# A fused decoder block on one core: the down bias moved into each expert's matmuls, the overflow table moved ahead of the last down projection, and three engines tied to the issue order

## The chip, the core and the metric

The kernel runs on one core of one Trainium2 chip. TensorE multiplies, VectorE (DVE in the rows) and ScalarE (ACT) do elementwise work, GpSimd (POOL) here issues the transfers that add into the output, and SyncE (SP) issues the loads of the weights. The metric is the device time of one execution in microseconds (us); lower is better.

## The reference

One decoder block on 512 tokens of width 1024, in float32: a gated linear recurrence and a sliding-window attention in parallel, merged and projected, and then a mixture of experts. The change touches only the experts:

```python
logits = xf @ w_router + b_router                  # 32 experts
top_vals, top_idx = lax.top_k(logits, 4)
gates = softmax(top_vals)
# for each expert e and the tokens xb that chose it:
hu = xb @ w_up[e] + b_up[e]                        # 1024 -> 2048
x_glu = minimum(hu[:, ::2], 7.0)
x_lin = clip(hu[:, 1::2], -7.0, 7.0)
act = x_glu * sigmoid(1.702 * x_glu) * (x_lin + 1.0)
y = act @ w_down[e] + b_down[e]                    # 1024 -> 1024
out[token] += g2 * gate[token, e] * y
```

All 32 experts' weights are read once: 256 MB (MB of 1024 KB here) of `w_up` and 128 MB of `w_down`, in float32.

## The kernel before, in words

The first 445 us or so hold the recurrence, the attention, the projections and the router. The rest, the stage of the experts, is a Python loop that is unrolled: at step `e` it runs the up projection of expert `e` and then the down projection of expert `e-1`.

A **weight tile** is 128 x 2048 float32 (1 MB). An expert has 12: up tiles k = 0 to 7 and down tiles j = 0 to 3. SyncE loads each into one of 12 slots. All but down tile 3 are then split in two float16 halves in one of 6 further slots: ScalarE writes the high half (L341), VectorE the low half (L342), and TensorE needs both. The names in the rows are those of the slots (`slot`, `slotb`, `slotc`, with a number), the split's target on the left of the arrow and the loaded tile on the right. The 6 targets go round, so the split of a tile waits until TensorE has finished with the sixth split tile before it. `ahead(i)` (L1044) issues the splits up to six tiles ahead of the matmuls.

For one expert TensorE runs, in the program's order: for k = 0 to 7 the 48 matmuls of `up_k` (L1139) on four PSUM banks `pu0` to `pu3`, in groups f = 0 to 15, four to a bank; ahead of k = 4, 5, 6 and 7 one of the four **select groups** (`pick`, L1100 and L1105: 16 matmuls each, the last with 4 more), which gather the tokens of the next expert with the 0/1 matrix `sel` that VectorE makes (L1119); then the down projection of the expert before, three tiles in float16 (L1175) and one in float32 (L1167), into `pd0` and `pd1`.

Between the two stand: `swiglu`, which takes the four banks through VectorE (L1148, L1150, L1151, L1155) and ScalarE (L1149, L1154) in two halves; `up_bias` (L1132), four ScalarE copies that write the up bias of the next expert into `pu0` to `pu3`, where the matmuls then add; and `finish`, in which VectorE scales the down result into the tile `y` (L1209, two operations) and GpSimd adds the rows of `y` into the output by an indirect transfer (L1179). `y` has one buffer.

The down bias of the kernel before is a product of its own. At step 27 `gates_T` transposes the gates of all tokens, and at steps 28 to 31, behind k = 1, `bias_rows` multiplies the gates of 128 tokens with the 32 rows of `b_down` (L1198, L1199), scales into `y` (L1200) and adds into the output. `overflow_table` makes, behind the last step but one, a table for experts with more than 96 tokens; the loop that reads it runs no iteration in these runs (`y` of L1209 is written 64 times, twice for each of 32 experts).

The order of each engine's instructions is not that of the program text: a scheduler sets it when the kernel is built, and each engine then takes its instructions in that order.

Of the kernel before, what the change touches and what calls it, by code (L numbers as in the profile page):

```python
# [21 lines left out]
D = 1024  # L22
# [19 lines left out]
def block_body(tc, x, c, positions, w_ada, b_ada, norm1_gain, w_in, lower_bound_logits, hg_norm_gain,  # L42
# [19 lines left out]
    with top:  # L62
# [869 lines left out]
        ge = moe.tile([128, NT, 2, NE], F32, name="ge")  # L932
# [66 lines left out]
        def gates(t):  # L999

            V.tensor_sub(gt[:, t], tv[:, t, 0:4], tv[:, t, 0:1].to_broadcast([128, 4]))
            A.activation(gt[:, t], gt[:, t], AF.Exp, accum_out=gs[:, t, 0:1])
            V.reciprocal(gs[:, t, 1:2], gs[:, t, 0:1])
            V.tensor_scalar(gt[:, t], gt[:, t], gs[:, t, 1:2], GS, op0=OP.mult, op1=OP.mult)
            V.tensor_mul(oh[:, t], oh[:, t], gt[:, t, :, None].to_broadcast([128, 4, NE]))
            V.tensor_reduce(ge[:, t, 0], oh[:, t].rearrange("p k e -> p e k"), axis=AX.X, op=OP.add)
            V.tensor_copy(aux[:, t, :, 1], ge[:, t, 0])
            V.tensor_sub(aux[:, t, :, 2], ge[:, t, 0], aux[:, t, :, 1])
            V.tensor_copy(ge[:, t, 1], ge[:, t, 0])
# [4 lines left out]
        SU = SW * SH2  # L1014

# [10 lines left out]
        def bias_dn():  # L1026
            st = ready.pop(("bdn",))
            A.activation(bd, st[:64, :1024], AF.Copy)
            V.tensor_sub(bd[32:64], st[32:64, :1024], bd[32:64])
            free(st)  # L1030
# [111 lines left out]
        def swiglu(hf, act, act32):  # L1142
            n = 4 * C
            gl, li = pu[hf][:, :n], pu[2 + hf][:, :n]
            g = moe.tile([128, n], F32, name="sg_g", bufs=2)
            s = moe.tile([128, n], F32, name="sg_s", bufs=2)
            l = act32.rearrange("p k c -> p (k c)") if hf else moe.tile([128, n], F32, name="sg_l", bufs=2)
            V.tensor_scalar(g, gl, 1.0 / SU, 7.0, op0=OP.mult, op1=OP.min)  # L1148
            A.activation(s, g, AF.Silu, scale=1.702)  # L1149
            V.tensor_scalar(l, li, -7.0 * SU, 7.0 * SU, op0=OP.max, op1=OP.min)  # L1150
            V.scalar_tensor_tensor(l, l, SU, s, op0=OP.add, op1=OP.mult)  # L1151
            nb = 2 if hf else 4
            hi, lo = (act[:, q, 4 * hf:4 * hf + nb].rearrange("p k c -> p (k c)") for q in range(2))
            A.activation(hi, l[:, :nb * C], AF.Copy, scale=SACT / SU)  # L1154
            V.scalar_tensor_tensor(lo, l[:, :nb * C], SACT / SU, hi, op0=OP.mult, op1=OP.subtract)  # L1155

        def new_act():

            return (moe.tile([128, 2, 6, C], F16, name="act", bufs=2),
                    moe.tile([128, 4, C], F32, name="act32", bufs=2))  # L1160

        def down_j(w, j, act, act32):
# [7 lines left out]
            for k in (2 * j, 2 * j + 1):  # L1170
                o = 1024 * (k % 2)
                for n, (pa_, pw) in enumerate(PASSES):
                    for u in range(2):
                        c0 = 2048 * pw + o + 512 * u
                        T.matmul(pd[u][:C, :], lhsT=act[:, pa_, k, :], rhs=w[:, c0:c0 + 512],  # L1175
                                 start=(k == 0 and n == 0), stop=False)
# [5 lines left out]

        gT = moe.tile([64, 2, S], F16, name="gT")

        def gates_T():

            for t in range(NT):
                T.transpose(pd[1][:64, 128 * t:128 * t + 128], ge[:, t].rearrange("p u e -> p (u e)"), ident)
            A.activation(gT[:, 0], pd[1][:64, :], AF.Copy)
            V.tensor_sub(gT[:32, 1], pd[1][:32, :], gT[:32, 0])  # L1190

        def bias_rows(t):

            tok = slice(128 * t, 128 * t + 128)
            y = moe.tile([128, D], F32, name="y")
            for u in range(2):
                sl = slice(512 * u, 512 * u + 512)
                T.matmul(pd[u], lhsT=gT[:, 0, tok], rhs=bd[:, sl], start=True, stop=False)  # L1198
                T.matmul(pd[u], lhsT=gT[:32, 1, tok], rhs=bd[:32, sl], start=False, stop=True)  # L1199
                V.scalar_tensor_tensor(y[:, sl], pd[u], 1.0 / GS, g2row[:, sl], op0=OP.mult, op1=OP.mult)  # L1200
            idx = moe.tile([128, 1], I32, name="idx", bufs=4)
            G.iota(idx, pattern=[[0, 1]], base=128 * t, channel_multiplier=1)
            add_out(y, idx, 128)
# [63 lines left out]
        open_banks()  # L1267
        first = prepare(0)
# [7 lines left out]
        for e in range(NEX + 1):  # L1276
            if e < NEX:
                xg, gate, idx = state[e]
                prep = prepare(e + 1) if e + 1 < NEX else iter(())
                for k in range(8):  # L1280
# [6 lines left out]
                    if k == 1 and e == NEX - NT - 1:  # L1287
                        gates_T()
                    if k == 1 and e >= NEX - NT:
                        bias_rows(e - (NEX - NT))  # L1290
            if e < NEX:
# [3 lines left out]
                for hf_ in range(2):  # L1295
                    swiglu(hf_, *acts[e])
            if e == 0:
                for b in range(4):
                    up_bias(bu[:, 1], b)
            if e > 0:  # L1300
                _, gate, idx = state.pop(e - 1)
                for j in range(4):
# [13 lines left out]
            if e == NEX - 1:  # L1316
                tables = overflow_table()
# [4 lines left out]
        with tc.For_i(0, nreg, 1) as it:  # L1322
# [39 lines left out]
            for hf_ in range(2):  # L1362
                swiglu(hf_, act, act32)
# [50 lines left out]
```

## Time and profile before

| what | value |
|---|---|
| median of 3 runs | 1549.35 us (1546.44 to 1549.44) |
| the profiled execution's own time | 1549.81 us |
| its span, first to last instruction | 1548.0 us |
| mean granted TensorE clock | 0.974 of full |
| busy share of the span | TensorE 91%, VectorE 84%, ScalarE 67%, GpSimd 17% |
| bytes moved by transfers | 478.54 MB, mean 309 GB/s over the span |

The profiled execution took 0.46 us more than the median, and 1.81 us more than its own span. In a row of the timeline the columns are the start in us, the duration (of the whole group, from the first start to the last end, where the row stands for several instructions), engine, line, operation, output and inputs, and the count; square brackets give the idle time ahead of it and what ended that.

### The profile page before, as it was taken

The numbers are of one execution on the slowest core, as the hardware profiler recorded it, in microseconds if no ns is written. First come the engines' busy times: TensorE is split into PE (matmuls) and PEld (weight loads), VectorE is DVE, ScalarE is ACT, GpSimd is POOL, SyncE is SP. The second block draws the span as 40 slices with busy tenths as digits, with TensorE's granted clock in tenths as the row PEclk, the third lists the DMA queues.
The fourth block names the chain that finished last, engine by engine and source line by source line (L and its number), as shares of the span: only waits on it lengthen the run. The fifth ranks groups of instructions, "written<-read, shape, count | busy, mean of one in ns | idle before, by whom it ended". The sixth has DMA issues, their size and how long they took to land. (4 is left out here: it accounts for less than half of the span.)

```text
span 1548.0 us, 41016 instructions
## 1 busy us (share of the span) xinstructions
PE 1405.2 (91%) x18156; PEld 1038.0 (67%) x18156; DVE 1299.1 (84%) x1470; ACT 1039.7 (67%) x1023; POOL 266.2 (17%) x89
## 2 busy tenths in 40 slices
PE   3979999999979999999999999999999999877675
PEld 2536566445468888788878877777777777666562
DVE  6876676867889999999989898989999989786765
ACT  4555335433469988888788787887877787755551
POOL 1020000011110462000334311112211112111221
PEclk9989999999989999999999999999999999988888
DMA  9812321667569999999999999999999999988761
GB/s 316 281 59 82 110 55 55 187 252 276 206 255 378 396 411 405 408 408 403 407 400 401 389 385 388 396 392 393 387 384 401 394 400 389 378 303 309 277 233 15
DMA packets 114096, 478.54 MB, mean 309 GB/s; under 512 B 10781, under 2 KB 35450, under 8 KB 81114
## 3 DMA queue, kind: packets, MB, share of 16 engines
q1 hardware_dynamic: 106160, 458.78, 76.2%
q0 software_dynamic: 6016, 14.82, 4.6%
q8 instruction: 144, 2.36, 0.6%
q10 hardware_dynamic: 1738, 2.27, 0.4%
q14 instruction: 38, 0.31, 0.1%
HBM read 463.22 MB, written 16.79 MB: 310 GB/s over the span
## 5 line engine op out<-in xcount | busy, mean ns | idle before, releaser
L1179 POOL DMA_INDIRECT out_dram<-y,idx x36 | 230.5, 6402 | 823.8 <-DVE y L1209 780.3
L1139 PE MATMUL pu<-xg,slot 128*128 128x96 f16 x6192 | 292.1, 208 | 36.1 <-DVE slot L342 30.6
L1139 PEld LDWEIGHTS <-slot 128*128 128x128 f16 x6192 | 277.3, 99 | 50.5 <-DVE slot L342 34.3
L342 DVE SCALAR_TENSOR_TENSOR slot<-slot,slot 128x2048 f16<-128x2048 f32 (+1 forms) x111 | 250.5, 2265 | 31.0 <-ACT slot L341 29.0
L341 ACT ACTIVATE slot<-slot 128x2048 f16<-128x2048 f32 (+1 forms) x111 | 222.8, 2025 | 47.5 <-DVE slot L342 23.6
L1175 PEld LDWEIGHTS <-act 128*96 128x96 f16 x1152 | 138.8, 123 | 122.2 <-issue 25.0
L1139 PE MATMUL pu<-xg,slotc 128*128 128x96 f16 x4032 | 187.8, 206 | 3.6 <-DVE slotc L342 2.2
L1139 PEld LDWEIGHTS <-slotc 128*128 128x128 f16 x4032 | 177.1, 98 | 13.1 <-issue 5.7
L695 PE MATMUL mm<-hT,slot 128*128 128x512 f16 x672 | 152.5, 382 | 0.0
L342 DVE SCALAR_TENSOR_TENSOR slot<-slotb,slot 128x2048 f16<-128x2048 f32 x61 | 138.7, 2283 | 2.0 <-ACT slot L341 2.0
L1175 PE MATMUL pd<-slot,act 128*96 128x512 f16 x552 | 127.9, 379 | 10.0 <-DVE slot L342 9.6
L342 DVE SCALAR_TENSOR_TENSOR slotc<-slot,slotc 128x2048 f16<-128x2048 f32 x56 | 127.3, 2283 | 10.8 <-ACT slotc L341 9.2
L341 ACT ACTIVATE slot<-slotb 128x2048 f16<-128x2048 f32 x61 | 118.8, 1950 | 2.1 <-ACT xg L1107 1.4
L1100 PE MATMUL gb<-sel,h 128*128 128x96 f16 x2048 | 119.0, 207 | 0.7 <-ACT xg L1107 0.5
L695 PEld LDWEIGHTS <-slot 128*128 128x128 f16 x672 | 65.9, 99 | 78.4 <-issue 4.4
L341 ACT ACTIVATE slotc<-slot 128x2048 f16<-128x2048 f32 x56 | 115.0, 2074 | 1.2 <-PE pu L1139 1.1
L1139 PE MATMUL pu<-xg,slotb 128*128 128x96 f16 x2064 | 100.4, 208 | 11.3 <-DVE slotb L342 9.8
L1100 PEld LDWEIGHTS <-h 128*128 128x128 f16 x2048 | 100.9, 99 | 9.4 <-issue 2.2
L1107 ACT ACTIVATE xg<-gb 128x384 f16<-128x384 f32 x128 | 61.7, 483 | 64.1 <-PE gb L1105 33.6
L1139 PEld LDWEIGHTS <-slotb 128*128 128x128 f16 x2064 | 93.0, 99 | 16.0 <-DVE slotb L342 10.8
L1175 PE MATMUL pd<-slotc,act 128*96 128x512 f16 x408 | 95.2, 379 | 7.6 <-DVE slotc L342 5.4
L1149 ACT ACTIVATE sg_s<-sg_g 128x384 f32<-128x384 f32 x64 | 33.2, 519 | 101.6 <-DVE sg_g L1148 101.2
(334 smaller groups left out, 2137.0 us busy)
## 6 DMA issues: line engine op xcount, KB each, us to landing
slot<-in_w_up_dram SPq DMA_DIRECT2D x164, 1024.0 KB
slotb<-in_w_down_dram SPq DMA_DIRECT2D x98, 1024.0 KB
slotc<-in_w_up_dram SPq DMA_DIRECT2D x62, 1024.0 KB
slotb<-in_w_up_dram SPq DMA_DIRECT2D x30, 1024.0 KB
slot<-in_w_down_dram SPq DMA_DIRECT2D x30, 1024.0 KB
slot<-in_w_in_dram SPq DMA_DIRECT2D x16, 1024.0 KB
slot<-in_w_ada_dram SPq DMA_DIRECT2D x16, 1024.0 KB
slot<-in_w_ada_dram SPq DMA_DIRECT2D x16, 512.0 KB
```

What stands on the lines that cost most here:

```text
L341: A.activation(hi, src, AF.Copy, scale=SW)
L342: V.scalar_tensor_tensor(lo, src, SW, hi, op0=OP.mult, op1=OP.subtract)
L695: T.matmul(bk, lhsT=hl[:, o:o + 128], rhs=hT[:, ph, k, :], start=(k == 0 and n == 0), stop=(k == KT - 1 and n == 2))
L1100: T.matmul(bk[:, C * k:C * k + C], lhsT=h2[:, part, t, 128 * kk:128 * kk + 128], rhs=sel[:, t, :], start=(k == 0 and t == 0), stop=(t == N ...
L1107: A.activation(xg[:, part, 4 * u:4 * u + 4, :].rearrange("p k c -> p (k c)"), bk[:, :4 * C], AF.Copy)
L1139: T.matmul(o, lhsT=hl[:, 2048 * pw + 128 * f:2048 * pw + 128 * f + 128], rhs=xg[:, pa_, k, :], start=False, stop=(k == KT - 1 and n == 2), ...
L1149: A.activation(s, g, AF.Silu, scale=1.702)
L1175: T.matmul(pd[u][:C, :], lhsT=act[:, pa_, k, :], rhs=w[:, c0:c0 + 512], start=(k == 0 and n == 0), stop=False)
L1179: G.indirect_dma_start(out=out2, out_offset=bass.IndirectOffsetOnAxis(ap=idx[:n, :1], axis=0), in_=y[:n, :], in_offset=None, bounds_check= ...
```

## The change

Four things are changed in the text; the matrix sizes, the weight tiles, their loads and the slots stay.

1. The down bias. `gates_T` and `bias_rows` are gone. In their place `down_bias` starts each expert's down projection with two matmuls (one for `pd0`, one for `pd1`): the stationary operand is a column of a one-hot matrix `E64`, spread over the 96 tokens, the moving one the bias in float16 high and low parts. `E64` is made once.
2. `swiglu` is one function for both halves and issues its VectorE operations next to each other: both `g`, both `l`, both products, both low halves.
3. The overflow table stands ahead of the last down projection.
4. From `open_banks()` to the end of the experts, each instruction of VectorE, ScalarE and TensorE is tied to the one issued before it on its engine, so that the scheduler keeps the order of the program text on these three.

```diff
+        E64 = moe.tile([64, NE], F16, name="E64")
+        V.tensor_scalar(E64, iota_e[:64, :], pmod[:, 0:1], 32768.0, op0=OP.is_equal, op1=OP.mult)
...
-        def swiglu(hf, act, act32):
+        def swiglu(act, act32):
...
+            for hf in range(2):
+                g.append(moe.tile([128, n], F32, name="sg_g", bufs=2))
+                V.tensor_scalar(g[hf], pu[hf][:, :n], 1.702 / SU, 7.0 * 1.702, op0=OP.mult, op1=OP.min)
+                s.append(moe.tile([128, n], F32, name="sg_s", bufs=2))
+                A.activation(s[hf], g[hf], AF.Silu)
+            for hf in range(2):
+                l.append(act32.rearrange("p k c -> p (k c)") if hf else moe.tile([128, n], F32, name="sg_l"))
+                V.tensor_scalar(l[hf], pu[2 + hf][:, :n], -7.0 * SU, 7.0 * SU, op0=OP.max, op1=OP.min)
+            parts = []
+            for hf in range(2):
+                V.scalar_tensor_tensor(l[hf], l[hf], SU, s[hf], op0=OP.add, op1=OP.mult)
...
+                A.activation(hi, l[hf][:, :nb * C], AF.Copy, scale=SACT / SU)
+                parts.append((lo, l[hf][:, :nb * C], hi))
+            for lo, src, hi in parts:
+                V.scalar_tensor_tensor(lo, src, SACT / SU, hi, op0=OP.mult, op1=OP.subtract)
...
+        def down_bias(one):
+            for u in range(2):
+                T.matmul(pd[u][:C, :], lhsT=one.to_broadcast([64, C]), rhs=bd[:, 512 * u:512 * u + 512],
+                         start=True, stop=False)
...
-        def gates_T():
...
-        def bias_rows(t):
...
+        traced = nc.cur_bb.bb.instructions
+        marks = {}
+        mark = traced[-1]
...
-                    if k == 1 and e == NEX - NT - 1:
-                        gates_T()
-                    if k == 1 and e >= NEX - NT:
-                        bias_rows(e - (NEX - NT))
...
-                for hf_ in range(2):
-                    swiglu(hf_, *acts[e])
+                swiglu(*acts[e])
...
+            if e == NEX:
+                tables = overflow_table()
             if e > 0:
                 _, gate, idx = state.pop(e - 1)
+                down_bias(E64[:, e - 1:e])
...
-            if e == NEX - 1:
-                tables = overflow_table()
+        begin = next(n for n in reversed(range(len(traced))) if traced[n] is mark) + 1
+        for ins in traced[begin:]:
+            eng = ins.engine
+            if eng in (V.engine, A.engine, T.engine):
+                if eng in marks:
+                    tc.add_manual_dep(ins, marks[eng].name, mybir.DependencyInfo(
+                        mybir.DependencyClass.NoSync, mybir.DependencyReason.DATA), reason="order")
+                marks[eng] = ins
```

What the built programs hold, at three places. **First place**: ScalarE around `swiglu` of expert 18. `sg_s` is the sigmoid product, `act` the high half for the down projection, `pu` the bias copy, `xg` the copy of a select group, and L341 the high half of a weight tile. Before:

```order
L1149 ACTIVATE sg_s_14325<-sg_g_14324 128x384
L1132 ACTIVATE pu0_3492<-bu_2868 128x384
L341 ACTIVATE slot2_65<-slotb2_2808 128x2048
L1107 ACTIVATE xg_14610<-gb_14613 128x384
L1132 ACTIVATE pu2_3494<-bu_2868 128x384
L1149 ACTIVATE sg_s_14334<-sg_g_14333 128x384
L1132 ACTIVATE pu1_3493<-bu_2868 128x384
L341 ACTIVATE slot4_67<-slotb3_2809 128x2048
L1154 ACTIVATE act_14322<-sg_l_14326 128x384
L1132 ACTIVATE pu3_3495<-bu_2868 128x384
```

And in the change:

```order
L341 ACTIVATE slotc1_3486<-slot7_70 128x2048
L1113 ACTIVATE xg_14073<-gb_14283 128x384
L1155 ACTIVATE sg_s_14360<-sg_g_14358 128x384
L1155 ACTIVATE sg_s_14364<-sg_g_14362 128x384
L1164 ACTIVATE act_14356<-sg_l_14366 128x384
L1164 ACTIVATE act_14356<-act32_14357 128x192
L341 ACTIVATE slotc3_3488<-slot3_66 128x2048
L1138 ACTIVATE pu0_3494<-bu_2868 128x384
L341 ACTIVATE slotb1_2807<-slotb4_2810 128x2048
L1138 ACTIVATE pu1_3495<-bu_2868 128x384
L341 ACTIVATE slot2_65<-slot1_64 128x2048
L1138 ACTIVATE pu2_3496<-bu_2868 128x384
```

Two rows follow in the same pattern, a fourth tile and the copy into `pu3`. Before, the four bias copies stood among the steps of `swiglu`, with two tiles between the first and the last; now they stand behind it, each behind one more tile, and the tile ahead of `swiglu` is, counted in the order of use, up tile 1 of the next expert.

**Second place**: VectorE around `y` of expert 16 before and 17 in the change. `sel` is the 0/1 matrix of the select groups, L342 the low half of a weight tile. Before:

```order
L342 SCALAR_TENSOR_TENSOR slotc1_3484<-slot8_71,slotc1_3484 128x2048
L1209 SCALAR_TENSOR_TENSOR y_13827<-pd0_3496,gate_12327,g2row_2221 96x512
L1209 SCALAR_TENSOR_TENSOR y_13827<-pd1_3497,gate_12327,g2row_2221 96x512
L342 SCALAR_TENSOR_TENSOR slotc3_3486<-slot0_63,slotc3_3486 128x2048
L1119 TENSOR_TENSOR sel_15077<-iota_c_2845,pos_2851 128x384
L342 SCALAR_TENSOR_TENSOR slotb1_2807<-slot7_70,slotb1_2807 128x2048
```

And in the change:

```order
L342 SCALAR_TENSOR_TENSOR slot4_67<-slot5_68,slot4_67 128x2048
L1204 SCALAR_TENSOR_TENSOR y_14434<-pd0_3498,gate_12928,g2row_2221 96x512
L1204 SCALAR_TENSOR_TENSOR y_14434<-pd1_3499,gate_12928,g2row_2221 96x512
L342 SCALAR_TENSOR_TENSOR slot6_69<-slotc0_3485,slot6_69 128x2048
L342 SCALAR_TENSOR_TENSOR slotc1_3486<-slotc2_3487,slotc1_3486 128x2048
L1125 TENSOR_TENSOR sel_14542<-iota_c_2845,pos_2851 128x384
L342 SCALAR_TENSOR_TENSOR slotc3_3488<-slotb0_2806,slotc3_3488 128x2048
```

Between `y` and `sel` there is now a second tile, and the `sel` behind `y` of expert 17 is that of expert 20, whose first select group comes in the same step. Before, the `sel` behind `y` of expert 16 was that of expert 21: it stood two experts further ahead.

**Third place**: ScalarE where the experts begin, behind the router's last exponential (`gt`). Before:

```order
L1002 ACTIVATE gt_2857,gs_2858<-gt_2857 128x4
L341 ACTIVATE slotc1_3484<-slotb0_2806 128x2048
L1132 ACTIVATE pu0_3492<-bu_2868 128x384
L1132 ACTIVATE pu1_3493<-bu_2868 128x384
L1132 ACTIVATE pu2_3494<-bu_2868 128x384
L1132 ACTIVATE pu3_3495<-bu_2868 128x384
L1107 ACTIVATE xg_3516<-gb_3519 128x384
L341 ACTIVATE slotc3_3486<-slotb1_2807 128x2048
```

And in the change:

```order
L1002 ACTIVATE gt_2857,gs_2858<-gt_2857 128x4
L1113 ACTIVATE xg_3516<-gb_3519 128x384
L1113 ACTIVATE xg_3516<-gb_3537 128x384
L1113 ACTIVATE xg_3516<-gb_3555 128x384
L1113 ACTIVATE xg_3516<-gb_3573 128x384
L1138 ACTIVATE pu0_3494<-bu_2868 128x384
L1138 ACTIVATE pu1_3495<-bu_2868 128x384
L1138 ACTIVATE pu2_3496<-bu_2868 128x384
L1138 ACTIVATE pu3_3497<-bu_2868 128x384
L341 ACTIVATE slotc1_3486<-slotb0_2806 128x2048
```

The first tile of the stage (three were split earlier) stood ahead of these eight copies and now stands behind them; on VectorE five such tiles then stand ahead of `sel` of expert 1.

On TensorE the select groups of an expert, which before were cut in pieces and spread over the down projection and the first up tiles, now stand whole ahead of k = 4, 5, 6 and 7.

## Rows read from the trace of the kernel before

**Rows 1.** Windows: PE, PEld, DVE, ACT, POOL busy, clock, DMA share, GB/s.

```profile
541.00:571.00 30.00, 30.00 (x491) 24.50 (x489) 30.00 (x27) 26.38 (x24) 17.39 (x1) 1.00 1.02 408
...
980.00:1013.00 33.00, 31.68 (x503) 25.24 (x500) 30.22 (x26) 26.48 (x24) 5.88 (x1) 1.00 1.00 392
```

**Rows 2.** The timeline of GpSimd: the add into the output that ends an expert.

```profile
512.49 17.49 POOL L1179 DMA_INDIRECT out_dram<-y,idx  x1 [67.16 <-DVE y L1209]
...
980.85 5.88 POOL L1179 DMA_INDIRECT out_dram<-y,idx  x1 [27.05 <-DVE y L1209]
...
1310.47 5.41 POOL L1179 DMA_INDIRECT out_dram<-y,idx  x1 [27.04 <-DVE y L1209]
...
1522.87 5.50 POOL L1179 DMA_INDIRECT out_dram<-y,idx  x1 [28.40 <-DVE y L1209]
1534.04 1.42 POOL L1179 DMA_INDIRECT out_dram<-y,idx  x1 [5.67 <-DVEq L1322]
```

**Rows 3.** The waits from 1388 to 1432 us: sum, times, longest.

```profile
DVE y L1200 <- DMA out_dram<-y,idx: 7.9, 1, 7.9
```

**Rows 4.** The timeline of TensorE, with the products of the down bias.

```profile
1345.28 0.39 PE L1199 MATMUL pd<-bd,gT 32*128 32x512 f16 x1
1345.60 0.39 PE L1198 MATMUL pd<-bd,gT 64*128 64x512 f16 x1
...
1361.28 3.70 PE L1139 MATMUL pu<-xg,slot 128*128 128x96 f16 x44 [9.52 <-DVE slot L342]
```

**Rows 5.** The timeline of TensorE early in the stage.

```profile
544.22 0.84 PE L1100 MATMUL gb<-sel,h 128*128 128x96 f16 x16
544.90 2.20 PE L1139 MATMUL pu<-xg,slotc 128*128 128x96 f16 x48
546.94 0.84 PE L1100 MATMUL gb<-sel,h 128*128 128x96 f16 x16
...
552.38 0.85 PE L1100 MATMUL gb<-sel,h 128*128 128x96 f16 x16
...
566.48 2.20 PE L1139 MATMUL pu<-xg,slotb 128*128 128x96 f16 x48
```

**Rows 6.** The timeline of VectorE in a steady period.

```profile
1012.10 1.40 DVE L1209 SCALAR_TENSOR_TENSOR y<-pd,gate,g2row 96x512 f32<-96x512 f32 x2
1013.42 2.27 DVE L342 SCALAR_TENSOR_TENSOR slotc<-slot,slotc 128x2048 f16<-128x2048 f32 x1
1015.62 0.55 DVE L1119 TENSOR_TENSOR sel<-iota_c,pos 128x384 f16<-128x384 f32 x1
1016.09 2.28 DVE L342 SCALAR_TENSOR_TENSOR slotb<-slot,slotb 128x2048 f16<-128x2048 f32 x1
1018.29 0.15 DVE L1111 TENSOR_SCALAR idx<-gb 96x1 int32<-96x1 f32 x1
...
1018.62 2.29 DVE L342 SCALAR_TENSOR_TENSOR slot<-slot,slot 128x2048 f16<-128x2048 f32 x1
```

**Rows 7.** The timeline of TensorE behind VectorE's tile of 1016.09.

```profile
1018.42 2.04 PE L1139 MATMUL pu<-xg,slotb 128*128 128x96 f16 x44 [0.29 <-DVE slotb L342]
```

**Rows 8.** The timeline of ScalarE in the same period.

```profile
1021.67 4.12 ACT L341 ACTIVATE slotc<-slotc 128x2048 f16<-128x2048 f32 x2
...
1034.06 0.48 ACT L1132 ACTIVATE pu<-bu 128x384 f32<-128x384 f32 x1
1034.47 0.51 ACT L1149 ACTIVATE sg_s<-sg_g 128x384 f32<-128x384 f32 x1
...
1040.49 0.36 ACT L1154 ACTIVATE act<-act 128x192 f16<-128x192 f32 x1 [0.60 <-DVE act L1151]
1040.76 2.04 ACT L341 ACTIVATE slot<-slot 128x2048 f16<-128x2048 f32 x1
```

**Rows 9.** The timeline of ScalarE where the stage begins.

```profile
453.19 0.49 ACT L1107 ACTIVATE xg<-gb 128x384 f16<-128x384 f32 x1 [0.69 <-PE gb L1105]
```

**Rows 10.** The first line of the page.

```profile
span 1548.0 us, 41016 instructions
```

More of the change, by code (lines that the diff above doesn't have):

```diff
@@ L931, in block_body @@
         gs = moe.tile([128, NT, 2], F32, name="gs")
-        ge = moe.tile([128, NT, 2, NE], F32, name="ge")
+        ge = moe.tile([128, NT, NE], F32, name="ge")
         GS = 1024.0
@@ L1005, in gates @@
             V.tensor_mul(oh[:, t], oh[:, t], gt[:, t, :, None].to_broadcast([128, 4, NE]))
[L1006 to L1009, printed above, removed]
+            V.tensor_reduce(ge[:, t, :], oh[:, t].rearrange("p k e -> p e k"), axis=AX.X, op=OP.add)
+            V.tensor_copy(aux[:, t, :, 1], ge[:, t, :])
+            V.tensor_sub(aux[:, t, :, 2], ge[:, t, :], aux[:, t, :, 1])
         bu = moe.tile([128, NE, 16], F32, name="bu")
@@ L1014, in block_body @@
         SU = SW * SH2
+        pmod = moe.tile([64, 1], F32, name="pmod")
+        G.iota(pmod[0:32], pattern=[[0, 1]], base=0, channel_multiplier=1, allow_small_or_imprecise_dtypes=True)
+        G.iota(pmod[32:64], pattern=[[0, 1]], base=0, channel_multiplier=1, allow_small_or_imprecise_dtypes=True)
+        E64 = moe.tile([64, NE], F16, name="E64")
+        V.tensor_scalar(E64, iota_e[:64, :], pmod[:, 0:1], 32768.0, op0=OP.is_equal, op1=OP.mult)
+        SBD = 1.702 * SW * SACT / 32768.0
         def bias_up():
@@ L1027, in bias_dn @@
             st = ready.pop(("bdn",))
-            A.activation(bd, st[:64, :1024], AF.Copy)
-            V.tensor_sub(bd[32:64], st[32:64, :1024], bd[32:64])
+            A.activation(bd, st[:64, :1024], AF.Copy, scale=SBD)
+            V.scalar_tensor_tensor(bd[32:64], st[32:64, :1024], SBD, bd[32:64], op0=OP.mult, op1=OP.subtract)
             free(st)
@@ L1140, in up_k @@
                              start=False, stop=(k == KT - 1 and n == 2), skip_group_check=True)
-        def swiglu(hf, act, act32):
+        def swiglu(act, act32):
             n = 4 * C
[L1144 to L1155, printed above, removed]
+            g, l, s = [], [], []
+            for hf in range(2):
[9 more added lines that the diff above has]
+                V.scalar_tensor_tensor(l[hf], l[hf], SU, s[hf], op0=OP.add, op1=OP.mult)
+                nb = 2 if hf else 4
+                hi, lo = (act[:, q, 4 * hf:4 * hf + nb].rearrange("p k c -> p (k c)") for q in range(2))
+                A.activation(hi, l[hf][:, :nb * C], AF.Copy, scale=SACT / SU)
+                parts.append((lo, l[hf][:, :nb * C], hi))
+            for lo, src, hi in parts:
+                V.scalar_tensor_tensor(lo, src, SACT / SU, hi, op0=OP.mult, op1=OP.subtract)
         def new_act():
@@ L1175, in down_j @@
                         T.matmul(pd[u][:C, :], lhsT=act[:, pa_, k, :], rhs=w[:, c0:c0 + 512],
-                                 start=(k == 0 and n == 0), stop=False)
+                                 start=False, stop=False)
         def add_out(y, idx, n):
@@ L1181, in add_out @@
                                  compute_op=OP.add)
-        gT = moe.tile([64, 2, S], F16, name="gT")
-        def gates_T():
[L1187 to L1190, printed above, removed]
-        def bias_rows(t):
[L1194 to L1203, printed above, removed]
         def finish(gate, idx):
@@ L1361, in block_body @@
                 hl_give(slot)
-            for hf_ in range(2):
-                swiglu(hf_, act, act32)
+            swiglu(act, act32)
+            e1h = moe.tile([64, 1], F16, name="ovh")
+            V.tensor_scalar(e1h, pmod, col[:64, 0:1], 32768.0, op0=OP.is_equal, op1=OP.mult)
+            down_bias(e1h)
             for j in range(4):
```

## The prediction

> **What bounds the kernel now.** I read first the timeline of GpSimd, because the add into the output marks the end of each expert [rows 2]: 512.49 us for expert 0, 980.85 for expert 15, 1310.47 for expert 25, 1522.87 for expert 30 and 1534.04 for expert 31. So the stage has three parts. The first 15 periods take 31.22 us each (468.36 / 15). The next ten take 32.96 (329.62 / 10). The five after those take 42.48 (212.40 / 5).
>
> The windows say what is full [rows 1]. In 33 us of a steady period TensorE is busy for 31.68, VectorE for 30.22, ScalarE for 26.48, and the transfers are at 392 GB/s of the 408 that they reach early in the stage. So four resources lie close together, and what an order of the work does to their waits can decide.
>
> TensorE's own period follows from two kinds of spacing [rows 5]. A select group with its up tile takes 2.72 (544.22 to 546.94), an up tile 2.04 (544.90 to 546.94). From the fourth select group to the next expert's first up tile it is 14.10 (552.38 to 566.48): 0.68 select, 2.04 tile, 11.38 down projection. One expert without any wait is then 14.10 + 4 x 2.04 + 3 x 2.72 = 30.42.
>
> The last five periods are long for another reason. The waits show VectorE's `y` of the down bias (L1200) held for 7.9 us by the transfer that empties the one buffer of `y` [rows 3]. The low halves of the tiles stand behind it, so TensorE then waits 9.52 us for one, and its next 44 matmuls take 3.70 us [rows 4], against 2.04 for 44 in a steady period [rows 7].
>
> **The change, part by part.**
>
> *The down bias.* What goes is the excess of five periods: 212.40 - 5 x 32.96 = 47.6 us. What comes is two matmuls of 512 columns for each expert. The nearest row is the old product's spacing, 0.32 us (1345.28 to 1345.60) [rows 4], so 0.64 for two, and TensorE's own period becomes 31.06. The bounds are nothing (hidden in a wait) and twice 0.39, the row's duration. In the order below the price falls into a wait, so it hardly moves the sum. [...] The other part, making `E64` and scaling the bias, is a handful of operations ahead of the stage, less than what `gates_T` drops.
>
> *The tie to the text's order with the new `swiglu`.* This moves most. I follow one period, with 0 at the start of an expert's fourth select group. A hand-over between engines costs 0.05 (VectorE's tile ends at 1016.09 + 2.28 = 1018.37 [rows 6], TensorE starts at 1018.42 [rows 7]). The spacings are: VectorE's tile 2.20, `y` 1.32, an operation of 128 x 384 0.47, the three small ones behind the selects 0.33 [rows 6]; ScalarE's tile 2.0 (two in 4.12, ends overlapping by 0.08), bias copy 0.41, the last, half-sized `act` 0.27 [rows 8].
>
> 1. ScalarE's tile ahead of `swiglu` is up tile 1 of the next expert. By the rotation of six targets it waits for TensorE's up tile 6, which ends at 0.16, so it runs from 0.20 to 2.30. VectorE's low half runs from 2.34 and frees VectorE at 4.54. The three small operations take it to 4.87.
> 2. Two `g`, two `l` and two products follow, 0.47 apart. The last product starts at 7.22 and ends at 7.77. ScalarE's last `act` starts at 7.81, and ScalarE is free at 8.08.
> 3. Now four tiles, each followed by one bias copy: 4 x 2.41 = 9.64. The fourth tile runs from 15.31 to about 17.40, its copy into `pu3` ends at 17.78. TensorE has begun the next expert's up tile 0 at 14.10 + 0.64 = 14.74 and needs `pu3` three quarters through it, at 14.74 + 1.53 = 16.27. It waits until 17.83: **1.56 us**. Before, these copies stood among the steps of `swiglu`, with two tiles between the first and the last: 1034.06 and 1034.47 show one of them directly ahead of the sigmoid [rows 8], so no such wait stood there.
> 4. VectorE's low half of that fourth tile runs from 17.45 to 19.65, `y` to 20.97, two tiles to 25.37, `sel` ends at 25.92. TensorE, free of `pu3` at 17.83, does the last quarter of up tile 0 (0.51) and tiles 1 to 3 (6.12), stands at the first select group at 24.46 and waits until 25.97: **1.51 us**. Before, `sel` came one tile behind `y` [rows 6] and two experts further ahead.
> 5. Three select groups with tiles, 8.16, bring it to the next fourth select group: a period of **34.13 us** = 31.06 + 1.56 + 1.51.
>
> In this chain VectorE and ScalarE aren't full: each waits for the other or for TensorE once a round, and the ring closes through the six targets. It is a fixed order, so the period holds from the first expert to the last with select groups.
>
> *The start.* ScalarE's last copy for expert 0's tokens ends at 453.68 [rows 9]. In the changed order four bias copies stand ahead of the stage's first tile (four starts, 1.6, to 455.3), that tile ends at 457.3, five low halves on VectorE (11.1 with the hand-over) reach 468.4, `sel` 468.9. Only then can the first select group of expert 1 run. Three more with their tiles, 8.16, set the first zero of the count above at 477.1. In this one round the four bias copies stand together behind `act` (8.08 + 4 x 0.41 = 9.72), the next tile's high half is done at 11.8, and three low halves and `sel` on VectorE end at 19.0; three selects more, and the next zero is 27.2 later, 504.3. From there the count holds, and `y` of expert 0 ends 21.0 behind that, at 525.3; its add starts at about 525.6, 13 us later than now [rows 2].
>
> *The table and the end.* Expert 30 has no selects ahead of it: from 17.83, one quarter tile 0.51, seven tiles 14.28, bias 0.64, down 11.38 and `y` 1.37 bring it to 46.0, which is 25.0 behind the `y` before. Expert 31's bias waits for the first half of that `y`, then 0.64 + 11.38 + `y` make it 12.8 later, where now it is 11.17 [rows 2]. The table's VectorE work lies beside that down projection, which is longer than it; if it stood in the way instead, some 5 us would come on top. From the last add to the end of the span, 13.96 (1548.0 [rows 10] less 1534.04 [rows 2]), stays.
>
> *The sum.* 525.6 + 29 x 34.13 (989.8) + 25.0 + 12.8 + 13.96 = 1567.2 of span. The profiled execution took 1.81 more than its span and 0.46 more than the median, so this is 1568.5 on the median's scale; I say **1568**. In other words: 25 periods lose about 2.2 each (55), the last five give back 50, the start loses 13, the end about 1. Break-even would be a period of 33.5.
>
> **The rivals.**
>
> *One of the two waits doesn't come* (the other side). The second, for `sel`, is a race of 1.5 us between eight VectorE operations and four tiles on TensorE. For it: a single tile done earlier by VectorE removes it. Against: every spacing in it is a row of a steady period. The period is then 32.62, the time 1568 - 29 x 1.51 = 1524. It decides from 0.64 us less a period on.
>
> *TensorE's own work sets the period*, 31.06, with both waits hidden by the reserve of six split tiles: 1568 - 29 x 3.07 = 1479. For it: TensorE is the busiest of the four [rows 1]. Against: in the new order no reserve is left, since the tile in step 1 waits for TensorE itself. [...]
>
> *The granted clock falls behind the new waits.* After 9.52 us of waiting 44 matmuls took 3.70 instead of 2.04 [rows 4, 7]. If each expert paid that once, it would be 1.66 x 29 = 48 on top, 1616. Against: after a wait of 0.29 the 44 ran at full speed [rows 7], and the clock is 1.00 in both windows [rows 1].
>
> **How the numbers follow.** A measurement of this kernel can tell about 0.2%, 3.1 us, from no change. The forecast has 0.70, its own range being 1556 to 1582 (0.4 us on a period). One wait fewer: 0.12. TensorE's own period: 0.07. The clock: 0.06. The last 0.05 is a shortening that happens to meet the break-even. Slower is then 0.76 (forecast and clock), faster 0.19, same 0.05. The range that keeps 8 in 10 leaves out the clock, TensorE's period and the far half of the first rival: 1538 to 1584.
>
> **What would show it.** In the changed profile the adds should be 34.1 apart from the first expert on, expert 0's at about 525. In each expert TensorE should show a wait of about 1.6 for a bias copy on ScalarE and one of about 1.5 for `sel`. The waits of 8 to 10 us in the last four experts should be gone, with the clock at 1.00 there, and the transfers should run below 392 GB/s. I am wrong if VectorE gets to `sel` earlier than 1.4 us behind TensorE, or if the bias copies come while up tile 0 is still in its third quarter.

## The result, and the profile after

The changed kernel takes 1568.97 us (median of 4 runs, 1568.66 to 1572.76) against 1547.89 of the kernel before: a ratio of 1.0142, 95% interval 1.0121 to 1.0163. The forecast was 1568, with 0.76 for slower. The profiled execution has a span of 1567.3 us; the sum of the prediction was 1567.2.

The timeline of GpSimd, as in [rows 2], for experts 0, 1, 14, 15, 25, 29, 30 and 31:

```profile
529.40 3.41 POOL L1196 DMA_INDIRECT out_dram<-y,idx  x1 [83.56 <-DVE y L1204]
563.47 10.31 POOL L1196 DMA_INDIRECT out_dram<-y,idx  x1 [30.65 <-DVE y L1204]
...
1005.81 10.30 POOL L1196 DMA_INDIRECT out_dram<-y,idx  x1 [23.70 <-DVE y L1204]
1039.78 10.29 POOL L1196 DMA_INDIRECT out_dram<-y,idx  x1 [23.67 <-DVE y L1204]
...
1380.28 10.29 POOL L1196 DMA_INDIRECT out_dram<-y,idx  x1 [23.71 <-DVE y L1204]
...
1516.85 1.42 POOL L1196 DMA_INDIRECT out_dram<-y,idx  x1 [23.72 <-DVE y L1204]
1541.84 1.42 POOL L1196 DMA_INDIRECT out_dram<-y,idx  x1 [23.57 <-DVE cnt L1215]
1554.38 1.42 POOL L1196 DMA_INDIRECT out_dram<-y,idx  x1 [11.12 <-DVEq L1326]
```

There are no stages left: the first period is 34.07 us, a later one 33.97, and 29 periods take 987.45, or 34.05 each (predicted 34.13). TensorE's waits over those 29 periods (529 to 1517 us; sum, times, longest) name two causes and hardly anything else:

```profile
PE gb L1106 <- DVE sel L1125: 39.1, 29, 1.4
PE pu L1145 <- ACT pu L1138: 35.0, 29, 1.3
PE gb L1106 <- issue: 0.4, 1, 0.4
PE pu L1145 <- issue: 0.4, 1, 0.4
```

The waits for a late low half that the last experts had before, of which [rows 4] shows one of 9.52, are gone, and the windows of the last experts show the clock at 1.00 with transfers at 370 to 388 GB/s (columns as in [rows 1]):

```profile
1380.00:1414.00 34.00, 31.45 (x504) 25.23 (x501) 30.57 (x27) 26.97 (x24) 10.29 (x1) 1.00 0.99 388
1414.00:1448.00 34.00, 31.01 (x489) 24.64 (x486) 29.94 (x25) 26.33 (x23) 10.30 (x1) 1.00 0.96 370
```

So the end gave back what was forecast and every period lost what was forecast. One period of TensorE, VectorE and ScalarE (their timelines; the fourth select group starts at 984.63, which is the zero of the prediction's count):

```profile
984.63 0.84 PE L1106 MATMUL gb<-sel,h 128*128 128x96 f16 x16
...
987.61 0.63 PE L1176 MATMUL pd<-bd,E 64*96 64x512 f16 x2
988.17 2.79 PE L1192 MATMUL pd<-slot,act 128*96 128x512 f16 x12
...
999.41 1.69 PE L1145 MATMUL pu<-xg,slotb 128*128 128x96 f16 x36
1002.32 0.67 PE L1145 MATMUL pu<-xg,slotb 128*128 128x96 f16 x12 [1.22 <-ACT pu L1138]
1002.83 6.30 PE L1145 MATMUL pu<-xg,slot 128*128 128x96 f16 x144
1010.46 0.85 PE L1106 MATMUL gb<-sel,h 128*128 128x96 f16 x16 [1.33 <-DVE sel L1125]
```

```profile
989.52 1.01 DVE L1153 TENSOR_SCALAR sg_g<-pu 128x384 f32<-128x384 f32 x2
...
994.77 4.67 DVE L342 SCALAR_TENSOR_TENSOR slot<-slot,slot 128x2048 f16<-128x2048 f32 x2 [1.43 <-ACT slot L341]
...
1004.13 1.40 DVE L1204 SCALAR_TENSOR_TENSOR y<-pd,gate,g2row 96x512 f32<-96x512 f32 x2
...
1009.85 0.55 DVE L1125 TENSOR_TENSOR sel<-iota_c,pos 128x384 f16<-128x384 f32 x1
```

```profile
992.69 2.05 ACT L341 ACTIVATE slot<-slot 128x2048 f16<-128x2048 f32 x1
...
1001.78 0.49 ACT L1138 ACTIVATE pu<-bu 128x384 f32<-128x384 f32 x1
```

From the zero, `g` starts at 4.89 (predicted 4.87), the first of the four tiles at 8.06 (8.08), the copy into `pu3` ends at 17.64 (17.78), TensorE goes on at 17.69 (17.83), `y` starts at 19.50 (19.65), `sel` ends at 25.77 (25.92), and the first select group starts at 25.83 (25.97). The waits in brackets are shorter than the predicted 1.56 and 1.51 because the page counts idle time from the end that it gives for the matmul before, which lies 0.16 behind the next start where nothing waits (544.90 + 2.20 against 546.94 in [rows 5]). From start to start they are 1.38 (1002.32 less 999.41 + 1.53) and 1.51 (1010.46 less 1002.83 + 6.12); the first is 0.18 shorter than predicted.

### The profile page after: what moved, and what is told of

It is laid out like the page before. It is cut to its first block, busy times and chain, and to the rows that moved or that the text cites. A ratio compares the mean times of both kernels' runs of the same rounds, so it can differ in the third digit from the quotient of the medians.

```text
span 1567.3 us, 41129 instructions
## 1 busy us (share of the span) xinstructions
PE 1406.7 (90%) x18200; PEld 1036.1 (66%) x18200; DVE 1310.0 (84%) x1458; ACT 1052.6 (67%) x1022; POOL 331.5 (21%) x83
## 5 line engine op out<-in xcount | busy, mean ns | idle before, releaser
L1196 POOL DMA_INDIRECT out_dram<-y,idx x32 | 296.0, 9249 | 814.0 <-DVE y L1204 779.3
L1145 PE MATMUL pu<-xg,slot 128*128 128x96 f16 x6192 | 283.2, 207 | 25.5 <-ACT pu L1138 25.1
L342 DVE SCALAR_TENSOR_TENSOR slot<-slot,slot 128x2048 f16<-128x2048 f32 (+1 forms) x111 | 252.0, 2272 | 55.3 <-ACT slot L341 51.4
L1145 PEld LDWEIGHTS <-slot 128*128 128x128 f16 x6192 | 272.0, 98 | 36.4 <-issue 33.8
L341 ACT ACTIVATE slot<-slot 128x2048 f16<-128x2048 f32 (+1 forms) x111 | 224.3, 2022 | 51.8 <-DVE slot L342 22.9
L1106 PE MATMUL gb<-sel,h 128*128 128x96 f16 x2048 | 109.2, 207 | 49.3 <-DVE sel L1125 48.8
L342 DVE SCALAR_TENSOR_TENSOR slotc<-slot,slotc 128x2048 f16<-128x2048 f32 x56 | 128.3, 2292 | 27.0 <-ACT slotc L341 24.5
L342 DVE SCALAR_TENSOR_TENSOR slot<-slotb,slot 128x2048 f16<-128x2048 f32 x61 | 138.6, 2286 | 13.2 <-ACT slot L341 12.0
L341 ACT ACTIVATE slot<-slotb 128x2048 f16<-128x2048 f32 x61 | 118.9, 1953 | 26.8 <-PE pu L1145 23.8
L1106 PEld LDWEIGHTS <-h 128*128 128x128 f16 x2048 | 94.4, 98 | 54.5 <-DVE sel L1125 53.3
L1192 PE MATMUL pd<-slot,act 128*96 128x512 f16 x552 | 123.9, 380 | 0.0
L341 ACT ACTIVATE slotc<-slot 128x2048 f16<-128x2048 f32 x56 | 116.2, 2075 | 8.5 <-PE pu L1145 8.5
L695 PEld LDWEIGHTS <-slot 128*128 128x128 f16 x672 | 65.7, 98 | 77.7 <-issue 3.1
L342 DVE SCALAR_TENSOR_TENSOR slotc<-slotb,slotc 128x2048 f16<-128x2048 f32 x42 | 95.5, 2286 | 12.7 <-ACT slotc L341 12.3
L1145 PE MATMUL pu<-xg,slotb 128*128 128x96 f16 x2064 | 95.7, 206 | 6.2 <-ACT pu L1138 6.1
L1184 PE MATMUL pd<-slot,act 128*96 128x512 f32 x216 | 97.1, 592 | 0.0
L341 ACT ACTIVATE slotc<-slotb 128x2048 f16<-128x2048 f32 x42 | 81.8, 1953 | 17.4 <-PE pu L1145 16.1
```

Of the source, the lines that this page charges most:

```text
L341: A.activation(hi, src, AF.Copy, scale=SW)
L342: V.scalar_tensor_tensor(lo, src, SW, hi, op0=OP.mult, op1=OP.subtract)
L695: T.matmul(bk, lhsT=hl[:, o:o + 128], rhs=hT[:, ph, k, :], start=(k == 0 and n == 0), stop=(k == KT - 1 and n == 2))
L1106: T.matmul(bk[:, C * k:C * k + C], lhsT=h2[:, part, t, 128 * kk:128 * kk + 128], rhs=sel[:, t, :], start=(k == 0 and t == 0), stop=(t == N ...
L1145: T.matmul(o, lhsT=hl[:, 2048 * pw + 128 * f:2048 * pw + 128 * f + 128], rhs=xg[:, pa_, k, :], start=False, stop=(k == KT - 1 and n == 2), ...
L1184: T.matmul(pd[u][:C, :], lhsT=act32[:, k - 4, :], rhs=w[:, o:o + 512], start=False, stop=(k == KT - 1))
```

## The experiments

The theory is the prediction's: VectorE and ScalarE in the fixed order form a ring with TensorE, that is a chain of waits that comes back to its start in each period, and TensorE waits twice in it. The rivals are that TensorE's own work, with the two new matmuls, or the transfers set the 34.0, and that each wait stands for itself. Each group of kernels was timed beside the kernel before on the same chip.

**`sel` first.**

```diff
-PICK_AT = (2, 4, 5, 6, 7)
+PICK_AT = (0, 4, 5, 6, 7)
```

> Changed kernel with one number altered: `sel` of the next expert is issued ahead of up tile 0 instead of up tile 2, so that on VectorE it stands directly behind `y`. Theory (one ring of VectorE and ScalarE in a fixed order, TensorE waiting twice in it, 1.2 us for a bias copy and 1.3 us for `sel`): `sel` ends at 21.5 of the period, ahead of the 24.5 at which TensorE asks for it, the second wait goes and the first stays; the period falls from 34.0 to 32.5 and the time from 1569 to about 1525. Rival (the two added matmuls or TensorE's own work set the period): no change, 1569. Rival (the ring is set elsewhere, the wait only moves): 1560 to 1569.

Measured: 1525.0 us, ratio 0.9867 (0.9843 to 0.9892). TensorE's waits over 29 periods (521 to 1472 us) now name `sel` no more, and the other wait stays:

```profile
PE pu L1145 <- ACT pu L1138: 26.7, 28, 1.3
PE pu L1145 <- issue: 7.6, 18, 0.9
```

The time falls by 44 us when one instruction of 0.55 us is moved, and the second wait goes. The period is 32.76 (521.51 to 1471.61), 1.29 shorter, which makes 37 of the 45 by which the spans of the two profiled executions differ (1567.3 and 1522.0). The other 8 lie ahead of the first add (521.51 against 529.40): there `sel` of expert 1 stands behind three low halves instead of five, and the stage itself began 2.4 earlier in this execution. TensorE's work and the added matmuls are the same in both kernels, so they don't set the 34.0.

**Bias copies first.**

```diff
-            if e == 0:
+            if e < NEX - 1:
                 for b in range(4):
-                    up_bias(bu[:, 1], b)
+                    up_bias(bu[:, e + 1], b)
...
-                    if e < NEX - 1:
-                        up_bias(bu[:, e + 1], j)
```

> Changed kernel with the four bias copies together, directly behind `swiglu` and ahead of the four tiles. Theory: the wait for the copies goes (the last one ends at 9.7 of the period and is wanted at 16.3), but the first of the four tiles is now done at 11.8 instead of 10.2, and VectorE, which has had nothing since 8.9, does its four low halves back to back to 20.6 instead of 19.65; `y`, two tiles and `sel` then end at 26.9, so the other wait grows to about 4 and the period by 1.0, to 35.0: about 1600. Rival (each wait costs what it shows and goes by itself): the period falls by 1.2 to 32.8, 1533.

Measured: 1669.65 us, ratio 1.0779 (1.0735 to 1.0823). The direction is the theory's and not the rival's: removing the wait for the copies makes the kernel slower. The size was missed by 70 us. TensorE's timeline and two windows show why:

```profile
986.64 1.46 PE L1106 MATMUL gb<-sel,h 128*128 128x96 f16 x16 [3.84 <-DVE sel L1125]
987.90 4.04 PE L1145 MATMUL pu<-xg,slotb 128*128 128x96 f16 x48
991.74 0.93 PE L1106 MATMUL gb<-sel,h 128*128 128x96 f16 x16
992.50 2.20 PE L1145 MATMUL pu<-xg,slot 128*128 128x96 f16 x48
...
997.26 0.84 PE L1106 MATMUL gb<-sel,h 128*128 128x96 f16 x16
...
1024.17 1.46 PE L1106 MATMUL gb<-sel,h 128*128 128x96 f16 x16 [3.81 <-DVE sel L1125]
```

```profile
986.60:988.00 1.40, 1.36 (x18) 1.36 (x19) 1.40 (x1) 0.00 (x0) 1.40 (x1) 0.50 1.02 433
988.00:992.00 4.00, 4.00 (x55) 4.00 (x53) 2.99 (x2) 0.51 (x2) 4.00 (x1) 0.51 1.01 426
```

The wait for `sel` is 3.84, about the 4 that was expected. The group behind it starts 26.91 after the fourth select group (997.26 to 1024.17), in the changed kernel 25.83: the ring itself grew by 1.08, as expected. Behind the wait the granted clock is 0.50 and 0.51 in the two windows, and the select group takes 1.46 instead of 0.84, the tile 4.04 instead of 2.20: 2.46 more in each period. Together that is 3.5, and the measured period is 37.57 (530.68 to 1620.29) against 34.05. So what the prediction's rival of the clock assumes does come in this kernel, behind 3.84 us of waiting; behind the 1.2 to 1.5 us in the changed kernel it doesn't, its mean clock over the 29 periods (529 to 1517 us) is 1.00. The 48 matmuls of the tile take 3.84 us from start to start behind the wait (987.90 to 991.74), 80 ns each, and 2.04 in the steady rows (544.90 to 546.94 in [rows 5]), 42.5 ns each.

**Untied, with the new and with the old `swiglu`; tied, with the old `swiglu`.** The first takes the tie out of the changed kernel:

```diff
...
-        for ins in traced[begin:]:
-            eng = ins.engine
-            if eng in (V.engine, A.engine, T.engine):
-                if eng in marks:
-                    tc.add_manual_dep(ins, marks[eng].name, mybir.DependencyInfo(
-                        mybir.DependencyClass.NoSync, mybir.DependencyReason.DATA), reason="order")
-                marks[eng] = ins
```

The other two issue each half of `swiglu` whole, with the new scales, without and with the tie:

```diff
-            for hf in range(2):
                 l.append(act32.rearrange("p k c -> p (k c)") if hf else moe.tile([128, n], F32, name="sg_l"))
                 V.tensor_scalar(l[hf], pu[2 + hf][:, :n], -7.0 * SU, 7.0 * SU, op0=OP.max, op1=OP.min)
-            parts = []
-            for hf in range(2):
                 V.scalar_tensor_tensor(l[hf], l[hf], SU, s[hf], op0=OP.add, op1=OP.mult)
...
-                parts.append((lo, l[hf][:, :nb * C], hi))
-            for lo, src, hi in parts:
-                V.scalar_tensor_tensor(lo, src, SACT / SU, hi, op0=OP.mult, op1=OP.subtract)
+                V.scalar_tensor_tensor(lo, l[hf][:, :nb * C], SACT / SU, hi, op0=OP.mult, op1=OP.subtract)
```

> Changed kernel without the tie to the text's order; the down bias in each expert's matmuls, the new `swiglu` and the table's place stay. Theory (the order costs the 2 us of each period): the order is close to that of before, so periods of 31 to 33 as there, and the five long periods at the end are gone: 1549 - 48 = about 1500. Rival (the bias matmuls cost their 0.6 us on the path): 1518. Rival (the new `swiglu` is what lengthens the period, tied or not): 1560.

> Only the down bias in the experts' matmuls and the table's place of the change: no tie, and `swiglu` half by half as before. Theory: the periods of before (31.2, then 33.0) all the way and no long ones at the end: 1546 - 48 = about 1500, so the new `swiglu` alone, without the tie, costs the 9 us between this and 1509. Rival (the bias matmuls cost them): 1509 to 1515.

> Changed kernel with `swiglu` half by half again as before (same scales), still tied to the text's order. Theory: in the fixed order VectorE then waits for ScalarE in each half, ScalarE is free for the next tiles at 9.6 of the period instead of 8.1, so the period grows by 1.5 to 35.5: 1569 + 44 = 1613. TensorE's wait for `sel` then is about 2.8; if the clock falls behind it as it did behind 3.84 us (the 16 select matmuls 1.46 instead of 0.84, the next 48 4.04 instead of 2.20), 2.4 a period come on top: 1680. Rival (the order inside `swiglu` doesn't matter): 1569.

| down bias in the experts | new `swiglu` | old `swiglu` |
|---|---|---|
| untied | 1509.1 us, 0.9748 (0.9727 to 0.9769) | 1511.86 us, 0.9762 (0.9733 to 0.9791) |
| tied | 1568.97 us, 1.0142 (1.0121 to 1.0163) | 1638.65 us, 1.058 (1.0555 to 1.0605) |

The tie costs 60 us with the new `swiglu` and 127 with the old. Of the 58 by which the profiled spans differ (1567.3 and 1509.6 with the new `swiglu`), 19 lie ahead of the first add (529.40 against 510.26) and 47 in the 29 periods; the last two experts give almost 9 back. The new `swiglu` gives nothing without the tie (the two medians differ by 0.2%) and 70 us with it. So neither the rival by which the new `swiglu` is what lengthens the period nor the one by which the order in it doesn't matter holds. The untied kernel with the new `swiglu`, at 1509.1, lies between the 1500 of the theory and the 1518 of the rival. The gain of the down bias and the table's place, untied and with the old `swiglu`, is 36 us, 12 less than the 48 that I expected, and the rival's 1509 to 1515 has the better number. In that kernel the 25 periods take 805.8 us (509.69 to 1315.52) where [rows 2] has 798.0, and one late period takes 36.67. Whether the two matmuls cost this or the somewhat different order that the scheduler then chose wasn't told apart.

In the tied kernel with the old `swiglu` some periods take 35.5, as the ring has it, and others 36.5 to 37.0. The longer wait isn't the one for `sel`, as I had it, which stays at 1.4 or less: it is the one for the bias copies, which now comes in two pieces. The windows of one of the longer periods:

```profile
1034.00:1042.00 8.00, 7.96 (x150) 7.81 (x147) 6.89 (x5) 6.00 (x4) 3.22 (x1) 0.79 1.01 399
1042.00:1050.00 8.00, 7.09 (x167) 7.10 (x168) 7.47 (x5) 6.02 (x5) 0.00 (x0) 1.00 1.00 372
```

This stretch stands behind two waits close together:

```profile
1031.21 0.67 PE L1145 MATMUL pu<-xg,slotb 128*128 128x96 f16 x12 [0.74 <-ACT pu L1138]
1033.57 0.67 PE L1145 MATMUL pu<-xg,slotb 128*128 128x96 f16 x12 [1.69 <-ACT pu L1138]
1034.07 7.88 PE L1145 MATMUL pu<-xg,slot 128*128 128x96 f16 x144
```

144 matmuls took 6.30 in the changed kernel, at a clock of 1.00; here, in the window at 0.79, they take 1.6 longer. One period later 0.92 and 1.73 of waiting were followed by 48 in 2.20, as in the steady rows of [rows 5], and 96 in 4.24, so in this kernel the matmuls slow down in some periods only. Of seven periods in a row (from the add at 1000.51 to the one at 1255.45), five take 36.55 to 37.01 and two 35.55 and 35.56; the 144 in 7.88 stand where two of the five meet, the 48 in 2.20 just ahead of one of the two. What decides between them isn't shown. My 2.4 for each period was too much: 1638.65 lies between the 1613 without it and the 1680 with it.

**Double bias.**

```diff
...
                 down_bias(E64[:, e - 1:e])
+                down_bias(E64[:, e - 1:e], False)
```

> Changed kernel with the two bias matmuls of each expert run twice (the output then holds the down bias twice). Theory (they lie in the time that TensorE waits for the bias copy anyway): the period stays at 34.0, that wait shrinks from 1.22 by 0.56 to about 0.66, only the last two experts get longer: 1569 to 1571. Rival (TensorE's work is the bound): 0.56 more in each period, 1586.

Measured: 1569.37 us, 0.4 from the changed kernel, with a period of 34.06 (529.05 to 1516.88). The second pair takes 0.43 (987.77 to 988.76 for both, 0.99, less 0.56 for one), not the 0.56 that I had, and TensorE's wait takes it back, 0.77 instead of 1.22:

```profile
987.77 1.06 PE L1176 MATMUL pd<-bd,E 64*96 64x512 f16 x4
988.76 2.79 PE L1192 MATMUL pd<-slot,act 128*96 128x512 f16 x12
...
1002.47 0.67 PE L1145 MATMUL pu<-xg,slotb 128*128 128x96 f16 x12 [0.77 <-ACT pu L1138]
```

**Late low half, two versions.** Both have `sel` first, and issue the low half of the tile ahead of up tile 7 behind `swiglu`. The core of the second (the first frees the source at the other end of the list of free slots):

```diff
-            V.scalar_tensor_tensor(lo, src, SW, hi, op0=OP.mult, op1=OP.subtract)
-            free(st)
+            low = lambda f: (V.scalar_tensor_tensor(lo, src, SW, hi, op0=OP.mult, op1=OP.subtract), free(st, f))
+            later[1].append(low) if later[0] else low(False)
...
-                    ahead(i)
+                    later[0] = k == 7; ahead(i); later[0] = False
...
-                swiglu(*acts[e])
+                swiglu(*acts[e]); [low(True) for low in later[1]]; later[1].clear()
```

> The kernel of the first run with one more edit: the low half of the tile that is split ahead of up tile 7 is issued on VectorE behind `swiglu` instead of ahead of it; its high half stays where it was. Theory: VectorE no longer waits there for a target that TensorE must free, so `swiglu` begins when TensorE's sums are there, at 2.9 instead of 4.9, ScalarE is through with the last bias copy at about 15.8, ahead of the 16.3 at which TensorE asks for it, and no wait of TensorE is left: its own period of 31.0, or what the transfers allow (12.9 MB at 408 GB/s are 31.5): 1475 to 1495. Rival (VectorE's 30 us of work in each period can't be packed closer than 32.5): 1525, as with `sel` alone.

> The kernel with the late low half, with one thing mended: there the tile's source came free later and was taken as the next split's target, so that ScalarE waited 2.84 us at 984.5 for VectorE's late low half. Here the freed source goes to the next load, and the six targets go round as in the changed kernel. Theory (fixed order of VectorE and ScalarE alone makes the waits): ScalarE is through with the bias copies before TensorE asks, no wait is left, the period is TensorE's 31.0 or the transfers' 31.5, the time 1475 to 1495. Rival (VectorE's 30 us of work can't be packed closer than 32.5): 1525. Rival (the transfers, at 393 GB/s in the run with `sel` alone, are at their end): 1510 to 1525.

The first took 1564.22 us, ratio 1.0108 (1.0089 to 1.0127), far from both expectations. ScalarE's timeline shows a new wait:

```profile
984.12 0.36 ACT L1164 ACTIVATE act<-act 128x192 f16<-128x192 f32 x1
987.32 2.04 ACT L341 ACTIVATE slot<-slot 128x2048 f16<-128x2048 f32 x1 [2.84 <-DMA slotb<-in_w_down_dram]
```

The row names a transfer, but VectorE's late low half runs from 984.95 to 987.24, 0.08 ahead of ScalarE's tile, and in most periods the profile names VectorE. ScalarE's waits from 540 to 1430 us have this one 26 times, 22 times with a low half (L342) as its end and 4 times with a transfer; two of the rows:

```profile
ACT slot L341 <- DVE slot L342: 25.5, 9, 2.8
...
ACT slot L341 <- DMA slotb<-in_w_down_dram: 11.3, 4, 2.8
```

In this kernel's order ScalarE's next tile writes into the slot that this low half reads, since that slot came free later and became the next target. The ring was closed again at another place. With the slots going round as before, the second version took 1507.95 us, ratio 0.9736 (0.9711 to 0.976), the fastest of the kernels that compute the whole output by its median, though the two untied ones lie within 0.3% of it. It is tied like the changed kernel, so a tie by itself need not cost the 60 us; the order that was written does. TensorE's waits from 540 to 1430, two of the rows:

```profile
PE pu L1145 <- ACT pu L1138: 8.8, 9, 1.7
PE pu L1145 <- issue: 7.6, 19, 0.9
```

In the same stretch the changed kernel waits 66 us for `sel` and the bias copies; 9 are left. The period is 32.03, under the rival's 32.5, so the engines can be packed closer; but it isn't 31.0 to 31.5.

**Fewer bytes.** In both kernels down tiles 1 and 2 are loaded by half:

```diff
+            n = 1 if j in (1, 2) else 2
             queue(("dn", e, j), lambda t: SP.dma_start(
-                t.rearrange("p (k f) -> p k f", k=2),
-                dview(w_down, (e * 1024 + 256 * j) * 1024, [[1024, 128], [128 * 1024, 2], [1, 1024]])))
+                t.rearrange("p (k f) -> p k f", k=2)[:, :n],
+                dview(w_down, (e * 1024 + 256 * j) * 1024, [[1024, 128], [128 * 1024, n], [1, 1024]])))
```

> The kernel of the mended late low half, with down tiles 1 and 2 of each expert loaded by half (the other half of the slot keeps what an earlier load left, so the output is not the reference's): 11.9 MB an expert instead of 12.9, all other work the same. Theory (with the waits gone the transfers are the bound: 32.07 us a period are 12.85 MB at the 401 GB/s measured there): the period falls to TensorE's own 31.0, 1508 - 29 x 1.05 = about 1478. Rival (VectorE and ScalarE can't be packed closer than 32): 1508.

> The changed kernel with the same two down tiles of each expert loaded by half. Theory (there the order's two waits are the bound, not the transfers, which run at 379 GB/s): the period stays at 34.0 and the time within 0.3% of 1569. Rival (the transfers set the 34.0, or late loads make the waits): 1569 - 29 x 1 to 2 = 1510 to 1540.

On the changed kernel: 1567.59 us, ratio 1.0134 (1.0117 to 1.0151), 0.1% from the full one, at 345 and 349 GB/s from 980 to 1014 and from 1300 to 1334 us, where the changed kernel has 372 and 390. The transfers have no part in its 34.0. On the late low half: 1493.42 us, ratio 0.9652 (0.9636 to 0.9668), half of the expected gain and between the theory's 1478 and the rival's 1508. The period falls from 32.03 to 31.79 only (518.30 to 1440.19); expert 30 then takes 25.7 instead of 29.5 and expert 31 12.5 instead of 15.1, so the loads held up the last two experts most. No wait for the bias copy is left there; what remains on TensorE is time for which the profile shows no cause:

```profile
PE pu L1146 <- issue: 8.0, 19, 0.9
PE gb L1107 <- issue: 4.2, 8, 1.4
PE pd L1177 <- issue: 1.1, 1, 1.1
```

That is 13.3 us in 28 periods, 0.48 each, of the 0.79 by which 31.79 exceeds 31.0. What the rest is, and what stands behind "issue", stays open. The profile also lists transfer queues of the kind "instruction" (86 and 18 packets, 1.41 and 0.15 MB from 700 to 1400 us), and no run here tells whether TensorE waited for them.

## Why the prediction was right

*What bounds the kernel.* The reading of the last five periods held for the changed kernel: they take 161.6 us (1380.28 to 1541.84), and the prediction's terms make 161.5 (four periods of 34.13 and 25.0). As a price of the down bias by itself the 47.6 is too much, since the untied kernels are only 36 to 37 us faster than the kernel before; where the rest goes was told apart only in part.

*The two matmuls.* They take 0.56, not 0.64, and fall into a wait as stated; doubling them changes nothing. It is the wait that makes them free; whether an order without one pays for them isn't shown.

*The tie and the ring.* Each step came within 0.15 us, the first wait within 0.18. That the period is set by this and not by work or transfers is shown by three runs: one `sel` moved shortens it by 1.29, 1 MB less for each expert gives 0.1% of the time, twice the bias gives nothing. What a wait is worth isn't read from the wait, but from what an edit does to the ring. The wait for `sel` could be taken out by itself. The one for the bias copies could not, by the edit tried: taken out of TensorE's way, the copies lengthened VectorE's part by 1.08, and the other wait grew by more than the one that went.

*The start.* The first add comes at 529.40, 3.8 later than worked out. Of this 2.1 is there at the fourth select group (479.21 against 477.1). TensorE's timeline and a window show the clock in it, which I left out of this place:

```profile
469.46 1.46 PE L1106 MATMUL gb<-sel,h 128*128 128x96 f16 x16 [8.70 <-DVE sel L1125]
470.72 3.21 PE L1145 MATMUL pu<-xg,slotc 128*128 128x96 f16 x48
...
488.43 4.00 PE L1145 MATMUL pu<-xg,slot 128*128 128x96 f16 x48 [6.18 <-ACT pu L1138]
```

```profile
469.00:474.00 5.00, 4.54 (x70) 4.54 (x71) 4.81 (x3) 1.47 (x3) 0.00 (x0) 0.61 1.03 416
488.40:492.20 3.80, 3.77 (x48) 3.77 (x48) 0.75 (x2) 3.17 (x4) 0.00 (x0) 0.50 0.01 2
```

`sel` itself ended at 469.40, 0.5 behind the 468.9 of the sum; the slower group and tile cost 0.58 and 1.01 more. The 0.5 is two errors that met: the stage's first low half starts at 455.64, 1.7 earlier than worked out, and VectorE then waits 2.10 for ScalarE between the five low halves, which the sum put back to back. The other 1.8 come in the round behind, which takes 29.0 (479.21 to 508.21) instead of 27.2. There VectorE waits 0.53 for the first sigmoid, ahead of which ScalarE has a row ACT_TABLE_LOAD of 1.28, and 0.73 and 0.30 between its low halves; the sum has none of the three. Against these 3.8 stand 2.3 in the 29 periods, 0.3 in the last expert (12.54) and 1.0 behind the last add (12.92 instead of 13.96). So the sum's agreement to 0.1 us is in part luck, errors of 4 us that met; the mechanism's size, 34.05 against 34.13, is not.

*The table.* Expert 31 ends 12.54 behind expert 30, as 12.8 had it with the table hidden.

*The rivals.* One wait fewer is what `sel` first makes, and its 1525.0 beside the 1524 that I gave is in part luck: the period is 32.76 instead of 32.62, 37 us of gain instead of 44, and the start, which this rival left as it was, gives 8 more. TensorE's own period isn't reached even where the waits are gone. The clock is 1.00 over the 29 periods of the changed kernel with their waits of 1.2 to 1.5 us, and 0.50 behind the 3.84 with the bias copies first.

## What to carry to other kernels

When engines are tied to a written order, follow one period instruction by instruction from rows of durations, and look for the place where the chain comes back to its start; for the period such a sum was good to 0.1 us here, and the shares of busy time (91, 84 and 67% before, 90, 84 and 67% after) hardly differ. In such a ring an instruction's place counts more than its length: moving `sel`, 0.55 us, gave 44 us, and moving copies out of one wait's way cost 101, of which the slower matmuls at a clock of 0.50 make 71 by my estimate (2.46 in each of 29 periods). And a buffer that is freed later may come back in another role: look at which slot the next writer gets before trusting an edit of the order.

## What the runs showed of the hardware

- TensorE's granted clock fell to 0.50 behind a wait of 3.84 us, with 16 + 48 matmuls in 1.46 and 4.04 us instead of 0.84 and 2.20, in the kernel with the bias copies first. In the changed kernel's start it was 0.50 behind one of 6.18 (48 in 4.00), and 0.61 over the 5 us around the end of one of 8.70. Over the 29 periods of the changed kernel, with waits of up to 1.4 us, its mean was 1.00 (529 to 1517 us). With the old `swiglu`, tied, it was 0.79 over 8 us behind two waits close together of 0.74 and 1.69; one period later, behind 0.92 and 1.73, 48 matmuls took 2.20 us.
- The two bias matmuls, 512 columns from 64 rows, took 0.28 us each from start to start, where the old product's row has 0.32; run twice, the second pair added 0.22 each.
- With fewer bytes to load and no wait for another engine TensorE still idled 13.3 us between 540 and 1430 us, for no cause that the profile shows.
